# A second feed-forward product by Strassen's identity over column pairs, row pairs and halves, with the residual kept in DRAM

## The chip, the core and the metric

The kernel runs on one NeuronCore of a Trainium2 chip. The metric is the device time of one execution in microseconds; the kernel before takes 2701.98 us (median of three runs, 2699.76 to 2704.55). Besides the runs that were timed there is one profiled execution, with every instruction's start and end.

## What is computed

A trunk of two layers works on x, 1024 frames by 1024 features, in float32. Layer 0 has a convolution module, layer 1 a chunkwise retention; each is followed by a feed-forward of 1024 to 4096 to 1024 features, and an RMS norm ends the trunk. Every sub-layer is normalized and modulated (shift, scale, gate) by a vector made of c. The part that matters here is the last feed-forward:

```python
h = modulate(rmsnorm(x, norm_mlp_g[i]), sh2, sc2)
x = x + g2[:, None, :] * (jnp.square(jax.nn.relu(h @ mlp_w1[i])) @ mlp_w2[i])
...
return rmsnorm(x, final_norm_g)
```

## The kernel before

**Layout.** Everything is held transposed: 128 features on the partitions, frames in the free dimension. x is eight rows of tiles (n = 0 to 7, of 128 features each) by two halves (t = 0 and 1, of 512 frames each), 128x512 apiece, in SBUF under the tags `x0` and `x1`.

**Products.** A float32 operand is split in two float32r tiles, hi (a cast by ScalarE) and lo (a subtraction by VectorE). A product of a 128x128 weight tile and a 128x512 tile is three matmuls into one PSUM bank: hi by hi, hi by lo, lo by hi (`mm3`, lines 258 to 260). `block` (lines 239 to 246) loads 128x1024 weights by SyncE into one of two `raw` buffers and splits them into two `whl` tiles.

**The feed-forward** (`mlp`, lines 416 to 454). The 4096 hidden features are eight blocks of 512. For each block the *first product* makes four hidden tiles for each half (eight times three matmuls each), squares their Relu (ScalarE and VectorE) and splits them (`split_pack`). The *second product* takes the block's four weight tiles of w2, one for each pair of columns (a column is 128 output features, n), and sums for each column and half four times three matmuls in PSUM. VectorE then adds the result, times the gate g2, to x in place (line 454). A block thus has 192 matmuls in each of its two products. PSUM has six buffers `mm` for products and two, `ax`, for norms.

**Order of the blocks in layer 1.** Block 0 runs for half 0 alone, then blocks 1 to 7 for both halves, then block 0 for half 1 alone: there, while the first product runs, the final norm of half 0 is done (`final`), and the second product is cut in 256 columns of frames (`mlp_split`, line 467), each of which is followed by its final norm. The norm of half 1 ahead of block 1 is made by `norm`.

**What sets the order.** The program names the operations in turn; a scheduler of the framework then places each engine's instructions by its own model of their times, and each engine runs its list in order. A tile gets one of the buffers of its tag, and waits for all that used that buffer before. The seven blocks' pools hold 8 `whl`, 16 `hB` (the h of half 1), and 5 each of `hid0` and `hid1`; `tmp` has 4 buffers.

Of the kernel before, what the change touches and what calls it, by code (L numbers as in the profile page):

```python
# [6 lines left out]
F32 = mybir.dt.float32  # L7
# [6 lines left out]
P = 128  # L14
# [192 lines left out]
class Trunk:  # L207
# [209 lines left out]
    def mlp(self, layer, sched, h, g2, mid=None, split=None):  # L417
        nc, io = self.nc, self.io
        for fb, halves in sched:
            hid = {t: [] for t in halves}  # L420
            for f in range(4):
                w = self.block(io["w1"][layer, fb * 4 + f])
                if self.bg:
                    self.bg.pop(0)()
                for t in halves:
                    ps = self.psum()
                    for kt in range(KT):
                        self.mm3(ps, w, kt * P, h[t][kt], kt == 0, kt == KT - 1)
# [3 lines left out]
                    nc.scalar.activation(rl, ps, AF.Relu)  # L432
                    sq = self.t2("tmp")
                    nc.vector.scalar_tensor_tensor(sq, ps, 0.0, rl, ALU.max, ALU.mult)
                    tag = self.hidtag[t]
                    hid[t].append(self.split_from(sq, *tag) if len(tag) == 2 else self.split_pack(sq, *tag))
            if mid is not None:
                mid()
            if split is not None:
                self.mlp_split(layer, fb, halves[0], hid[halves[0]], g2, split)  # L440
                continue
            for np_ in range(4):
                w = self.block(io["w2"][layer, fb, np_])
                if self.bg:
                    self.bg.pop(0)()
                for n2 in range(2):
                    n = np_ * 2 + n2
                    for t in halves:
                        ps = self.psum()
                        for kt in range(4):  # L450
                            o = kt * 256 + n2 * P
                            self.mm3(ps, w, o, hid[t][kt], kt == 0, kt == 3)
                        x = self.x[n][t]
                        nc.vector.scalar_tensor_tensor(x, ps, g2[:, n : n + 1], x, ALU.mult, ALU.add)  # L454

    def mlp_split(self, layer, fb, t, hid, g2, done):

        nc = self.nc
        ws = [self.block(self.io["w2"][layer, fb, np_]) for np_ in range(4)]
        for cs in (slice(0, MID), slice(MID, HALF)):  # L460
            for n in range(KT):
                ps = self.psum()[:, :MID]
                for kt in range(4):
                    o = kt * 256 + n % 2 * P
                    self.mm3(ps, ws[n // 2], o, [a[:, cs] for a in hid[kt]], kt == 0, kt == 3)
                x = self.x[n][t][:, cs]
                nc.vector.scalar_tensor_tensor(x, ps, g2[:, n : n + 1], x, ALU.mult, ALU.add)
            done(t, cs)


    def layer_conv(self):
# [324 lines left out]
        def mlp(fb, p):  # L796
            h = hcols("m0")
            hid = []
            for f in range(4):
                name, ps = ("w1", fb, f), ("psm", fb, f)  # L800
                for kt in range(KT):
                    mm(ps, name, kt * P, h[kt], kt == 0, kt == KT - 1, p)
                rl, hd = ("rl", fb, f), ("hid", fb, f)
                op("A", 0.478, p, lambda ps=ps, rl=rl: nc.scalar.activation(E[rl], E[ps], AF.Relu), r=[ps], w=[rl], a={rl: ("tmp", {})})
                op("V", 0.602, p, lambda ps=ps, rl=rl: nc.vector.scalar_tensor_tensor(E[ps], E[ps], 0.0, E[rl], ALU.max, ALU.mult),
                   r=[rl], w=[ps])
                op("A", 0.478, p, lambda ps=ps, hd=hd: nc.scalar.copy(E[hd][:, :HALF], E[ps]), r=[ps], w=[hd],
                   a={hd: ("hid0", dict(dt=F32R, cols=2 * HALF))})
# [351 lines left out]
    def run(self):  # L1160
        nc, io, tc, main, ctx = self.nc, self.io, self.tc, self.main, self.ctx
        self.x = [[None, None] for _ in range(KT)]
        self.tags = {"raw": (main, RINGS["raw"]), "tmp": (main, RINGS["tmp"]), "rs": (main, 1), "hA": (main, 16),
                     "x0": (main, 8), "x1": (main, 8), "sm": (main, 6)}
        modp = tc.tile_pool(name="modp", bufs=1)
        mp = modp.__enter__()
        self.tags.update(cond=(mp, 1), araw=(mp, RINGS["araw"]))
        self.constants()
        with tc.tile_pool(name="g0", bufs=1) as gp:
            self.tags.update(hB=(gp, 16), hid0=(gp, RINGS["hid0"]), whl=(gp, RINGS["whl"]))  # L1170
            with ExitStack() as self.cstack, tc.tile_pool(name="psc", bufs=1, space=PSUM) as self.ps:
                self.psb = {"mm": 4, "ax": 1, "acc": 3}
                self.hidtag = {0: ["hid0"]}
                hm, g2 = self.layer_conv()
            psp = tc.tile_pool(name="ps", bufs=1, space=PSUM, reuse_waits="tile")
            self.ps = ctx.enter_context(psp)
            self.psb = {"mm": 6, "ax": 2}
            with tc.tile_pool(name="hid", bufs=1) as hp:
                self.tags["hid1"] = (hp, 4)
                self.hidtag = {0: ["hid0"], 1: ["hid1"]}  # L1180
                h, (sh1, G1, g1, sh2, G2, g2) = self.layer_mlp0(hm, g2)
        modp.__exit__(None, None, None)
        with tc.tile_pool(name="ret", bufs=1, reuse_waits="tile") as rp, tc.tile_pool(name="dp", bufs=1, space=bass.MemoryType.DRAM) as dp:
# [7 lines left out]
            self.mlp(1, [(0, [0])], hm, g2, mid=out)  # L1191
        with tc.tile_pool(name="g1", bufs=1, reuse_waits="tile") as gp:
            self.tags.update(whl=(gp, 8), hB=(gp, 16), hid0=(gp, 5), hid1=(gp, 5))
            self.hidtag = {0: ["hid0"], 1: ["hid1"]}
            hm[1] = self.norm(1, G2, sh2, "hB")
            self.mlp(1, [(fb, [0, 1]) for fb in range(1, 8)], hm, g2)

            def first():
                self.tagname = {"tmp": "hid0", "xg": "hA"}
                self.final(0)  # L1200
                self.tagname = {}

# [35 lines left out]
def lay_out(i):  # L1238
# [11 lines left out]
    def kblocks(w):  # L1250

        k, nn = w.shape
        return w.reshape(k // 512, 4, P, 4, 256).transpose(0, 3, 2, 1, 4).reshape(k // 512, 4, P, 1024)

    vec = np.zeros((P, NVEC), np.float32)

    def put(name, a):
# [29 lines left out]
        "w2": c(np.stack([kblocks(w) for w in i["mlp_w2"]])),  # L1287
    }
    d.update(constants_np())
    return d  # L1290
# [23 lines left out]
```

## Time and profile before

| | us |
|---|---|
| runs timed | 2699.76, 2701.98, 2704.55 |
| the profiled execution | 2705.48 |
| its span, first to last instruction | 2703.6 |
| TensorE busy | 2613.8 (97%) |
| VectorE busy | 1635.2 (60%) |
| ScalarE busy | 1068.3 (40%) |
| GpSimd busy | 314.5 (12%) |

The mean granted TensorE clock is 0.985. In the profile PE is TensorE, PEld its weight loads, DVE is VectorE, ACT ScalarE, POOL GpSimd, SP SyncE. A row of the groups reads: line, engine, operation, output and inputs, shapes, count, then busy time and the mean duration in ns, then the idle time of the engine just before and what ended it. A row of the windows gives the stretch and, for each engine, busy time and count. A row of the timeline begins with the start, in us from the first instruction, and the duration. Matmuls are pipelined, so that a matmul's own duration is longer than its share of the time; the distance of starts counts.

### The profile page before, as it was taken

What the parts mean: (1) busy time and instruction counts of PE and PEld (TensorE: products, weight loads), DVE (VectorE), ACT (ScalarE), POOL (GpSimd) and SP (SyncE); (2) the same over time, 40 slices, a digit from 0 to 9 for tenths busy, and PEclk for the clock granted to TensorE, in tenths of its full rate; (3) what the DMA queues carried; (4) which work ended last, traced back from release to release, by engine and by line L of the source; (5) the groups of instructions that cost most, each with busy time, mean ns of one, the idle gap of its engine ahead of it and who ended that gap; (6) DMA issues with size and microseconds to landing.
All of it is one profiled execution on the core that took longest, in us unless ns stands there. A gap on an engine that the chain in (4) does not pass through costs nothing.

```text
span 2703.6 us, 29259 instructions
## 1 busy us (share of the span) xinstructions
PE 2613.8 (97%) x11450; PEld 2119.2 (78%) x11450; DVE 1635.2 (60%) x2237; ACT 1068.3 (40%) x1582; POOL 314.5 (12%) x212
## 2 busy tenths in 40 slices
PE   2989999999999999999999999999999999999997
PEld 1756777888787888788888888888888888888886
DVE  7799999965577445645545655365565333333336
ACT  4656866463222323343433633433543211222124
POOL 3677439100000000000000000000000000000002
PEclk6999999999999999999999999999999999999999
DMA  7522322242376223322222232232222111111112
GB/s 253 203 71 86 109 93 87 93 128 98 119 233 217 96 94 96 115 86 94 71 94 94 71 103 85 71 101 86 78 70 71 48 54 47 47 47 47 48 54 86
DMA packets 77197, 259.66 MB, mean 96 GB/s; under 512 B 8577, under 2 KB 11009, under 8 KB 76930
## 3 DMA queue, kind: packets, MB, share of 16 engines
q1 hardware_dynamic: 74240, 252.98, 28.6%
q10 hardware_dynamic: 2818, 4.81, 0.5%
q8 instruction: 90, 1.47, 0.2%
q14 instruction: 49, 0.40, 0.0%
HBM read 251.46 MB, written 6.29 MB: 95 GB/s over the span
## 4 chain that ended last, share of the span: by engine, by line
PE 84%; DVE 7%; DMA 4%; ACT 2%; issue 2%; POOL 1%; DVEq 0%; ACTq 0%; SPq 0%; POOLq 0%
PE mm L260 25%; PE mm L259 25%; PE mm L258 25%; DMA araw<-ada 3%; PE mm L964 2%; PE mm L963 2%; PE mm L962 2%; DVE acc L733 1%; POOL cacc L741 1%; DVE whl L523 1%; DVE araw L319 1%; PE ax L606 1%; PE acc L721 1%; DVE araw L555 0%; DVE hid L555 0%
## 5 line engine op out<-in xcount | busy, mean ns | idle before, releaser
L245 ACT CAST whl<-raw 128x1024 fp32r<-128x1024 f32 x264 | 277.0, 1050 | 809.7 <-PE mm L259 472.3
L246 DVE TENSOR_TENSOR whl<-raw,whl 128x1024 fp32r<-128x1024 f32 x264 | 322.7, 1223 | 403.5 <-ACT whl L245 302.7
L258 PE MATMUL mm<-hA,whl 128*128 128x512 f32 x1200 | 483.2, 403 | 44.5 <-ACT whl L522 41.7
L260 PE MATMUL mm<-hA,whl 128*128 128x512 f32 x1200 | 475.5, 396 | 8.5 <-DVE whl L523 6.3
L259 PE MATMUL mm<-hA,whl 128*128 128x512 f32 x1200 | 476.1, 397 | 1.9 <-DVE hA L542 1.7
L258 PE MATMUL mm<-hid,whl 128*128 128x512 f32 (+1 forms) x1024 | 394.3, 386 | 4.6 <-ACT hid L281 3.0
L259 PE MATMUL mm<-hid,whl 128*128 128x512 f32 (+1 forms) x1024 | 392.8, 384 | 1.1 <-DVE hid L282 1.0
L260 PE MATMUL mm<-hid,whl 128*128 128x512 f32 (+1 forms) x1024 | 392.8, 384 | 0.0
L258 PEld LDWEIGHTS mm<-hA,whl 128*128 128x128 f32 x1200 | 227.7, 190 | 101.3 <-ACT whl L522 43.5
L258 PE MATMUL mm<-hB,whl 128*128 128x512 f32 x704 | 279.3, 397 | 0.0
L260 PEld LDWEIGHTS mm<-hA,whl 128*128 128x128 f32 x1200 | 227.5, 190 | 63.8 <-DVE whl L523 9.8
L259 PE MATMUL mm<-hB,whl 128*128 128x512 f32 x704 | 274.4, 390 | 0.0
L260 PE MATMUL mm<-hB,whl 128*128 128x512 f32 x704 | 274.2, 390 | 0.0
L259 PEld LDWEIGHTS mm<-hA,whl 128*128 128x128 f32 x1200 | 227.6, 190 | 58.7 <-issue 5.3
L454 DVE SCALAR_TENSOR_TENSOR x<-mm,modb,x 128x512 f32<-128x512 f32 x192 | 143.8, 749 | 211.6 <-PE mm L260 211.0
L741 POOL TENSOR_TENSOR cacc<-cacc,prod 128x512 f32<-128x512 f32 x166 | 253.4, 1529 | 112.9 <-ACT prod L738 57.9
L1143 POOL TENSOR_SCALAR hA<-x,vec 128x256 f32<-128x256 f32 (+1 forms) x12 | 7.5, 622 | 2164.3 <-DVE x L454 2143.8
L258 PEld LDWEIGHTS mm<-hid,whl 128*128 128x128 f32 x1024 | 192.9, 189 | 45.6 <-ACT hid L281 5.9
L259 PEld LDWEIGHTS mm<-hid,whl 128*128 128x128 f32 x1024 | 192.9, 188 | 41.3 <-DVE hid L282 2.9
L260 PEld LDWEIGHTS mm<-hid,whl 128*128 128x128 f32 x1024 | 193.1, 189 | 37.1
L733 DVE SCALAR_TENSOR_TENSOR acc<-x,vec,acc 128x512 f32<-128x512 f32 x239 | 166.8, 746 | 2.8 <-PE acc L721 1.9
L259 PEld LDWEIGHTS mm<-hB,whl 128*128 128x128 f32 x704 | 132.2, 188 | 31.3 <-issue 2.9
(233 smaller groups left out, 3776.3 us busy)
## 6 DMA issues: line engine op xcount, KB each, us to landing
raw<-w SPq DMA_DIRECT2D x192, 512.0 KB, 3.5
araw<-ada SPq DMA_DIRECT2D x80, 512.0 KB, 4.3
raw<-pw SPq DMA_DIRECT2D x38, 512.0 KB, 4.1
raw<-rqk SPq DMA_DIRECT2D x32, 512.0 KB, 3.5
raw<-rv SPq DMA_DIRECT2D x32, 512.0 KB, 3.5
raw<-rgate SPq DMA_DIRECT2D x32, 512.0 KB, 3.5
raw<-rout SPq DMA_DIRECT2D x32, 512.0 KB, 3.5
x<-x SPq DMA_DIRECT2D x32, 256.0 KB, 3.2
```

What stands on the lines that cost most here:

```text
L245: nc.scalar.copy(hi[i], raw[:, i * W : i * W + W])
L246: nc.vector.tensor_tensor(lo[i], raw[:, i * W : i * W + W], hi[i].bitcast(F32), ALU.subtract)
L258: nc.tensor.matmul(out, whi, rhi, start=start, stop=False)
L259: nc.tensor.matmul(out, whi, rlo, start=False, stop=False)
L260: self.last_mm = nc.tensor.matmul(out, wlo, rhi, start=False, stop=stop)
L319: i = nc.vector.scalar_tensor_tensor(raw, raw, 1.0, self.cond, ALU.mult, ALU.mult, accum_out=out)
L454: nc.vector.scalar_tensor_tensor(x, ps, g2[:, n : n + 1], x, ALU.mult, ALU.add)
L733: op("V", 0.68, p, lambda s=s, a=a: nc.vector.scalar_tensor_tensor(E[a], sl(s), wv(s), E[a], ALU.mult, ALU.add), r=[u], w=[a])
L741: op("G", 1.28, p, lambda pr=pr: nc.gpsimd.tensor_tensor(E[ca], E[ca], E[pr], ALU.add), r=[pr], w=[ca])
L962: nc.tensor.matmul(vps[jt], hh[0], wh, start=kt == 0, stop=False)
L963: nc.tensor.matmul(vps[jt], hh[0], wl, start=False, stop=False)
L964: nc.tensor.matmul(vps[jt], hh[1], wh, start=False, stop=kt == KT - 1)
```

## The change

In blocks 1 to 7 of the last feed-forward the second product is no longer a sum of plain products. Take a pair of output columns (n1, n2), a pair of hidden tiles (kj = 0, 1) and the two halves: that is a 2x2 by 2x2 product of tiles, and in place of its eight products seven are made, of sums and differences:

A11·B11, A12·B21, S2·T2, S1·T1, S4·B22, S3·T3, A22·T4.

- `pair_weights` loads a column pair's weights (laid out anew by `kpairs`), makes S1 to S4 on VectorE and splits them all: four `whl` tiles a pair.
- In `mlp_seven` the hidden tiles' Relu is done by ScalarE in PSUM and the Square by ScalarE into buffers of `x0`; VectorE makes T1 to T4, and seven tiles of each pair of hidden tiles are split.
- `seven` runs the products over the two pairs of hidden tiles (six matmuls each, in one PSUM bank). The results are gathered, times g2, in tiles of `tmp`: ScalarE makes two (a and b) from the first product, VectorE adds the others, eight additions a pair.
- x no longer lies in SBUF during these blocks: it is stored to DRAM tiles `xd` at the start by SyncE, and each finished 128x512 tile is added to it by a transfer that GpSimd issues (`accum_op=ALU.add`), four a pair. After block 7 it is loaded back: half 0 by SyncE, half 1 by ScalarE's queue.
- Buffers: `whl` 9, `hB` 8 (the other half of half 1's h takes buffers of `x1`), `hid0` 14, a new `q2`.
- `o2` only gives the place of a weight tile in the new layout, for the blocks that are done as before.

The core of the diff:

```diff
+    def pair_weights(self, ap):
+        nc = self.nc
+        tt = nc.vector.tensor_tensor
+        raw = self.t2("raw", cols=1024)
+        nc.sync.dma_start(raw, ap)
+        a11, a12, a21, a22 = (raw[:, i * 256 : i * 256 + 256] for i in range(4))
+        ph, pl, qh, ql = (self.t2("whl", dt=F32R, cols=1024) for _ in range(4))
+        q = self.t2("q2")
+        tt(q[:, 256:], a11, a21, ALU.subtract)
+        nc.scalar.copy(qh[:, 512:768], a22)
+        tt(ql[:, 512:768], a22, qh[:, 512:768].bitcast(F32), ALU.subtract)
+        tt(a21, a21, a22, ALU.add)
+        tt(a22, a21, a11, ALU.subtract)
+        tt(q[:, :256], a12, a22, ALU.subtract)
+        nc.scalar.copy(ph, raw)
+        tt(pl, raw, ph.bitcast(F32), ALU.subtract)
+        nc.scalar.copy(qh[:, :512], q)
+        tt(ql[:, :512], q, qh[:, :512].bitcast(F32), ALU.subtract)
...
+    def seven(self, np_, w, hid, g2, xd):
...
+        def plus(ps, n, e, new=False):
+            o = self.t2("tmp") if new else e
+            nc.vector.scalar_tensor_tensor(o, ps, g(n), e, ALU.mult, ALU.add)
+            return o
+        def done(n, t, e):
+            nc.gpsimd.dma_start(xd[n][t], e, accum_op=ALU.add)
+        ps = prod("A11", "B11")
+        a, b = self.t2("tmp"), self.t2("tmp")
+        nc.scalar.activation(a, ps, AF.Copy, scale=g(n1))
+        nc.scalar.activation(b, ps, AF.Copy, scale=g(n2))
+        done(n1, 0, plus(prod("A12", "B21"), n1, a, True))
+        ps = prod("S2", "T2")
+        plus(ps, n1, a)
+        plus(ps, n2, b)
+        m5 = prod("S1", "T1")
+        plus(m5, n1, a)
+        plus(prod("S4", "B22"), n1, a)
+        done(n1, 1, a)
+        plus(prod("S3", "T3"), n2, b)
+        done(n2, 1, plus(m5, n2, b, True))
+        plus(prod("A22", "T4"), n2, b)
+        done(n2, 0, b)
...
+                        nc.scalar.activation(ps, ps, AF.Relu)
+                        sq = f[kj, t] = self.t2("x0")
+                        nc.scalar.activation(sq, ps, AF.Square)
...
-            self.tags.update(whl=(gp, 8), hB=(gp, 16), hid0=(gp, 5), hid1=(gp, 5))
-            self.hidtag = {0: ["hid0"], 1: ["hid1"]}
-            hm[1] = self.norm(1, G2, sh2, "hB")
-            self.mlp(1, [(fb, [0, 1]) for fb in range(1, 8)], hm, g2)
+            self.tags.update(whl=(gp, 9), hB=(gp, 8), hid0=(gp, 14), q2=(gp, 1))
...
+            for kt in range(KT):
+                nc.sync.dma_start(xd[kt][1], self.x[kt][1])
+                h.append(self.norm_h(1, kt, r, G2[:, kt : kt + 1], sh2[:, kt : kt + 1], "hB" if kt < 4 else "x1"))
...
+                nc.sync.dma_start(xd[kt][0], self.x[kt][0])
+            self.mlp_seven(1, range(1, 8), hm, g2, xd)
...
+                nc.sync.dma_start(self.x[kt][0], xd[kt][0])
...
+                nc.scalar.dma_start(self.x[kt][1], xd[kt][1])
```

Lines of the changed kernel that the prediction names: 497 is `plus`, 505 and 506 the two copies of the first product, 501 the adding transfer, 469 to 478 the weights' sums and splits, 1234 the final norm's sum of squares (1132 before), 569 the addition in `mlp_split` (467 before), 439 and 287 the square and the split of a hidden tile in `mlp` (434 and 282 before). The order of an engine's instructions is shown with each tile's number, in the form line, operation, output<-inputs, shape.

More of the change, by code (lines that the diff above doesn't have):

```diff
@@ L28, with o2 @@
 VEC = {}
+def o2(kt, n):
+    return (n % 2 * 4 + kt % 2 * 2 + kt // 2) * P
 def _vec_layout():
@@ new lines, in seven, with prod @@
+    def seven(self, np_, w, hid, g2, xd):
+        nc = self.nc
+        n1, n2 = 2 * np_, 2 * np_ + 1
+        g = lambda n: g2[:, n : n + 1]
+        def prod(a, k):
+            ps = self.psum()
+            wt, o = w[a]
+            for p in range(2):
+                self.mm3(ps, wt, o + p * P, hid[p][k], p == 0, p == 1)
+            return ps
+        def plus(ps, n, e, new=False):
[20 more added lines that the diff above has]
+        done(n2, 0, b)
@@ new lines, in mlp_seven @@
+    def mlp_seven(self, layer, fbs, h, g2, xd):
+        nc, io = self.nc, self.io
+        tt = nc.vector.tensor_tensor
+        for fb in fbs:
+            hid = []
+            for p in range(2):
+                f = {}
+                ops = {}
+                pack = lambda k, src: ops.update({k: self.split_pack(src, "hid0")})
+                for kj in range(2):
+                    w = self.block(io["w1"][layer, fb * 4 + 2 * p + kj])
+                    for t in range(2):
+                        ps = self.psum()
+                        for kt in range(KT):
+                            self.mm3(ps, w, kt * P, h[t][kt], kt == 0, kt == KT - 1)
+                        nc.scalar.activation(ps, ps, AF.Relu)
+                        sq = f[kj, t] = self.t2("x0")
+                        nc.scalar.activation(sq, ps, AF.Square)
+                        if (kj, t) == (0, 0):
+                            pack("B11", sq)
+                        elif (kj, t) == (0, 1):
+                            tt(f[0, 0], sq, f[0, 0], ALU.subtract)
+                            pack("T1", f[0, 0])
+                        elif (kj, t) == (1, 0):
+                            pack("B21", sq)
+                        else:
+                            pack("B22", sq)
+                            tt(f[0, 0], sq, f[0, 0], ALU.subtract)
+                            pack("T2", f[0, 0])
+                            tt(f[0, 1], sq, f[0, 1], ALU.subtract)
+                            pack("T3", f[0, 1])
+                            tt(f[1, 0], f[1, 0], f[0, 0], ALU.subtract)
+                            pack("T4", f[1, 0])
+                hid.append(ops)
+            for np_ in range(4):
+                self.seven(np_, self.pair_weights(io["w2"][layer, fb, np_]), hid, g2, xd)
@@ L463, in mlp_split @@
                 for kt in range(4):
-                    o = kt * 256 + n % 2 * P
-                    self.mm3(ps, ws[n // 2], o, [a[:, cs] for a in hid[kt]], kt == 0, kt == 3)
+                    self.mm3(ps, ws[n // 2], o2(kt, n), [a[:, cs] for a in hid[kt]], kt == 0, kt == 3)
                 x = self.x[n][t][:, cs]
@@ L1191, in run @@
             self.mlp(1, [(0, [0])], hm, g2, mid=out)
+        xp = ctx.enter_context(tc.tile_pool(name="xd", bufs=1, space=bass.MemoryType.DRAM))
         with tc.tile_pool(name="g1", bufs=1, reuse_waits="tile") as gp:
-            self.tags.update(whl=(gp, 8), hB=(gp, 16), hid0=(gp, 5), hid1=(gp, 5))
-            self.hidtag = {0: ["hid0"], 1: ["hid1"]}
-            hm[1] = self.norm(1, G2, sh2, "hB")
-            self.mlp(1, [(fb, [0, 1]) for fb in range(1, 8)], hm, g2)
+            self.tags.update(whl=(gp, 9), hB=(gp, 8), hid0=(gp, 14), q2=(gp, 1))
+            self.hidtag = {1: ["hid0"]}
+            xd = [[xp.tile([P, HALF], F32, name=self.nm("xd"), tag=f"xd{n}_{t}") for t in range(2)] for n in range(KT)]
+            r = self.norm_rstd(1)
+            h = []
+            for kt in range(KT):
+                nc.sync.dma_start(xd[kt][1], self.x[kt][1])
+                h.append(self.norm_h(1, kt, r, G2[:, kt : kt + 1], sh2[:, kt : kt + 1], "hB" if kt < 4 else "x1"))
+            hm[1] = h
+            for kt in range(KT):
+                nc.sync.dma_start(xd[kt][0], self.x[kt][0])
+            self.mlp_seven(1, range(1, 8), hm, g2, xd)
+            xl = [self.t2("hid0", cols=2 * HALF) for _ in range(4)]
+            for kt in range(KT):
+                self.x[kt][0] = self.t2("x0")
+                nc.sync.dma_start(self.x[kt][0], xd[kt][0])
+            for kt in range(KT):
+                self.x[kt][1] = xl[kt // 2][:, kt % 2 * HALF : kt % 2 * HALF + HALF]
+                nc.scalar.dma_start(self.x[kt][1], xd[kt][1])
             def first():
@@ L1286, in lay_out @@
         "w1": c(np.stack([ktiles(w, 0) for w in i["mlp_w1"]])),
-        "w2": c(np.stack([kblocks(w) for w in i["mlp_w2"]])),
+        "w2": c(np.stack([kpairs(w) for w in i["mlp_w2"]])),
     }
```

10 lines of the change are left out of this document (7 added, 3 removed).

## Prediction

> **What bounds the kernel now.** I read the page first: the shares of the engines and the chain that ended last.
>
> ```profile
> PE 2613.8 (97%) x11450; PEld 2119.2 (78%) x11450; DVE 1635.2 (60%) x2237; ACT 1068.3 (40%) x1582; POOL 314.5 (12%) x212
> ...
> PE 84%; DVE 7%; DMA 4%; ACT 2%; issue 2%; POOL 1%; DVEq 0%; ACTq 0%; SPq 0%; POOLq 0%
> ```
>
> TensorE is the bound almost everywhere. Then the stage itself, by windows: one second product and the first product after it, in the middle of the seven blocks, then the last block's first product (half 1 alone) and the end.
>
> ```profile
> core 0: us, PE busy (x) PEld busy (x) DVE busy (x) ACT busy (x) POOL busy (x), PEclk, DMA share, GB/s
> 2071.50:2115.00 43.50, 43.50 (x193) 36.02 (x193) 17.36 (x21) 5.31 (x6) 0.00 (x0) 1.00 0.16 49
> 2115.00:2159.20 44.20, 44.20 (x193) 36.05 (x193) 15.07 (x19) 12.43 (x18) 0.00 (x0) 1.00 0.15 48
> 2641.30:2663.00 21.70, 21.70 (x97) 18.00 (x96) 11.86 (x15) 9.86 (x14) 0.00 (x0) 1.00 0.23 73
> 2663.00:2703.60 40.60, 26.87 (x203) 24.89 (x202) 30.05 (x50) 16.17 (x36) 13.74 (x14) 0.91 0.30 105
> ```
>
> In the blocks PE has no gap and the full granted clock; VectorE is at 34 to 40%, GpSimd idle. Only the last 40.6 us are not PE's: there VectorE is busy for 30.05.
>
> **The gain.** A second product is 192 matmuls (the 193 counts one that straddles the edge) in 43.5 us, 0.2267 us each. The change runs 7 of 8 products: 4 column pairs x 42 = 168 per block, 24 fewer, 168 fewer over seven blocks: 168 x 0.2267 = **38.1 us**. A product of six matmuls takes 1.36 us, a column pair 9.52, a block's second product 38.1. First products stay.
>
> **What VectorE gets.** Prices from the rows of the stage (busy) and from a dense stretch elsewhere (start to start):
>
> ```profile
> L454 DVE SCALAR_TENSOR_TENSOR x<-mm,modb,x 128x512 f32<-128x512 f32 x96 | 72.0, 750 | 150.0 <-PE mm L260 149.8
> L246 DVE TENSOR_TENSOR whl<-raw,whl 128x1024 fp32r<-128x1024 f32 x50 | 61.2, 1225 | 95.6 <-ACT whl L245 92.8
> L282 DVE TENSOR_TENSOR hid<-tmp,hid 128x512 fp32r<-128x512 f32 x50 | 34.6, 691 | 30.2 <-ACT hid L281 30.2
> L281 ACT CAST hid<-tmp 128x512 fp32r<-128x512 f32 x50 | 31.0, 621 | 53.7 <-DVE tmp L434 53.7
> L432 ACT ACTIVATE tmp<-mm 128x512 f32<-128x512 f32 x51 | 30.4, 596 | 72.1 <-PE mm L260 72.1
> ```
>
> ```profile
> 1560.89 0.68 DVE L270 TENSOR_TENSOR q<-tmp,q 128x512 fp32r<-128x512 f32 x1
> 1561.49 0.68 DVE L917 TENSOR_TENSOR tmp<-mm,cs 128x512 f32<-128x512 f32 x1
> ...
> 1564.49 0.74 DVE L1082 SCALAR_TENSOR_TENSOR x<-mm,modb,x 128x512 f32<-128x512 f32 x1
> 1565.15 0.68 DVE L270 TENSOR_TENSOR k<-tmp,k 128x512 fp32r<-128x512 f32 x1
> ...
> 1569.27 1.22 DVE L246 TENSOR_TENSOR whl<-raw,whl 128x1024 fp32r<-128x1024 f32 x1
> 1570.40 1.28 DVE L270 TENSOR_TENSOR st<-tmp,st 128x512 fp32r<-128x512 f32 x2
> ```
>
> ```profile
> L374 DVE TENSOR_TENSOR rs<-hid,hid 128x256 f32<-128x256 f32 x2 | 0.8, 424 | 0.2
> ```
>
> Back to back, instructions overlap: an addition of a product 0.66 us, a 512-column operation 0.60, a 1024-column one 1.13; a 256-column one 0.34 (0.42 less the same overlap, an estimate). A column pair now needs 8 additions (5.28) where it had 4, and for its weights 1.13 + 0.60 + 5 x 0.34 = 3.43 where it had 1.13: **8.7 us of VectorE for 9.52 of PE**. That fits, with little to spare. The first product, 44.2 us of PE, carries 14 splits and 8 differences of 0.60, two pairs' weights and little else, some 22 us. ScalarE has per pair two copies of a product (0.6 each) and 2 us of casts: hidden.
>
> At the turn from first to second product T2 of the last hidden tile is late: Relu and square (0.6 each), difference 0.66, cast 0.62, low part 0.69, with one copy ahead of the cast in ScalarE's order, about 4.2 us; PE comes to it after three products, 4.1 us. I put 0.3 us a block: **2 us**.
>
> **The wait that is added.** A finished tile leaves through a transfer issued by GpSimd that adds to DRAM; its `tmp` buffer, one of four, is free when that has landed. Of VectorE's order around a pair's end, before (two columns of two halves each):
>
> ```order
> L454 SCALAR_TENSOR_TENSOR x1_912_4310<-mm_3287_16278,modb_1523_7887,x1_912_4310 128x512
> L246 TENSOR_TENSOR whl_3315_16489<-raw_3313_16486,whl_3314_16488 128x1024
> L454 SCALAR_TENSOR_TENSOR x0_515_2224<-mm_3291_16298,modb_1523_7887,x0_515_2224 128x512
> L454 SCALAR_TENSOR_TENSOR x1_913_4319<-mm_3292_16312,modb_1523_7887,x1_913_4319 128x512
> L454 SCALAR_TENSOR_TENSOR x0_518_2233<-mm_3293_16326,modb_1523_7887,x0_518_2233 128x512
> ```
>
> And now, from the second pair's end into the third (tmp_3578, written first, is the tile whose buffer tmp_3590 takes):
>
> ```order
> L497 SCALAR_TENSOR_TENSOR tmp_3578_17750<-mm_3575_17725,modb_1523_7887,tmp_3571_17703 128x512
> L473 TENSOR_TENSOR raw_3597_17846<-raw_3597_17846 128x256
> L497 SCALAR_TENSOR_TENSOR tmp_3571_17703<-mm_3579_17753,modb_1523_7887,tmp_3571_17703 128x512
> L474 TENSOR_TENSOR q2_3602_17852<-raw_3597_17846 128x256
> L476 TENSOR_TENSOR whl_3599_17849<-raw_3597_17846,whl_3598_17848 128x1024
> L497 SCALAR_TENSOR_TENSOR tmp_3590_17797<-mm_3589_17790,modb_1523_7887,tmp_3587_17786 128x512
> L478 TENSOR_TENSOR whl_3601_17851<-q2_3602_17852,whl_3600_17850 128x512
> ```
>
> Between the tile and the one that needs its buffer lie 0.34 + 0.66 + 0.34 + 1.13 = 2.5 us of work. Call L the time from the end of the addition to the buffer's release. No row of before shows a GpSimd transfer or one that adds; the nearest, of the same 256 KB:
>
> ```profile
> raw<-w SPq DMA_DIRECT2D x192, 512.0 KB, 3.5
> ...
> std<-tmp SPq DMA_DIRECT2D x8, 256.0 KB, 2.0
> tmp<-std SPq DMA_DIRECT2D x8, 256.0 KB, 2.6
> ```
>
> ```profile
> 2249.26 0.33 SPq L239 DMA_DIRECT2D raw<-w  x1
> ```
>
> ```profile
> L1151 POOL TENSOR_TENSOR hA<-hA,rs 128x512 f32<-128x512 f32 x3 | 4.7, 1593 | 27.7 <-DVE rs L374 27.7
> ```
>
> Lower end: a plain store, 2.0, issued in 0.33, and 0.15 for the semaphore: 2.5 us. Upper end: a load and then a store, 4.6, and GpSimd as long over the issue as over its 1.59 us operation: 6.3. I take 4.2, near the middle: the read and the write of different rows overlap.
>
> How much L may be: let t = 0 be PE's end of the first product. After Relu and Square VectorE starts at 1.5 on three differences, four low parts (two of which wait for casts), a 256-column operation and the first addition; they end at 6.9. Six more additions of 0.66 end at 10.9: there the first pair's last new tile is complete. Pair 2 can begin at 10.9 + L (for L over 3), needs 7 x 0.66 + 3 x 0.34 = 5.7 to its own last new tile; pair 3, with two weight blocks of 1.13 among its additions, 7.5. So pair 4's first addition begins at 10.9 + 5.7 + 7.5 + 3L = 24.1 + 3L and frees its PSUM buffer at 24.8 + 3L. PE has six PSUM buffers; it wants that one for the next block at 28 x 1.36 + 0.2 = 38.3. **L up to 4.5 us costs nothing; every us beyond costs 3 us a block, 21 us in all.** At 4.2 I leave 0.4 us a block for transfers that land late: **3 us**.
>
> "DMA: Bandwidth & Descriptors" of the Trainium skill, section "Anatomy of one DMA — SWDGE (gpsimd) path", gives 2.0 us + bytes/436e3, by which 256 KB take 2.6 us (an estimate; it speaks of plain transfers) and the ring would cost 0; no run so far shows it.
>
> **The two seams.** At the start, 16 stores of x stand among SyncE's weight loads; the second weight tile waits only for columns 0 and 1, done 15 us earlier, the third for the block's end, 22 us ahead of its use. Half 1's h partly lies in buffers of x: half a first-product group may run at another pace (rival 3): **1 us**. At the end the residual of half 0 comes back by loads, and its final norm, which ran beside the last first product, moves behind it. VectorE before, from the last hidden tile:
>
> ```order
> L434 SCALAR_TENSOR_TENSOR tmp_3688_19203<-mm_3686_19176,tmp_3687_19201 128x512
> L370 SCALAR_TENSOR_TENSOR hid0_3717_19263<-ax_3690_19208,hid0_3716_19261 128x512
> L282 TENSOR_TENSOR hid1_3689_19205<-tmp_3688_19203,hid1_3689_19205 128x512
> L372 TENSOR_SCALAR hid0_3718_19265<-hid0_3717_19263 128x512
> L374 TENSOR_TENSOR rs_3719_19267<-hid0_3718_19265,hid0_3715_19259 128x512
> ```
>
> And now: the sums of squares (L1234) only begin there.
>
> ```order
> L439 SCALAR_TENSOR_TENSOR tmp_3982_20007<-mm_3980_19980,tmp_3981_20005 128x512
> L287 TENSOR_TENSOR hid0_3983_20009<-tmp_3982_20007,hid0_3983_20009 128x512
> L1234 TENSOR_TENSOR hid0_3987_20017<-hid0_3985_20013,hid0_3986_20015 128x512
> L569 SCALAR_TENSOR_TENSOR hid0_3944_19832<-mm_4026_20113,modb_1523_7887,hid0_3944_19832 128x256
> L1234 TENSOR_TENSOR hid0_3989_20021<-hid0_3987_20017,hid0_3988_20019 128x512
> ```
>
> ```profile
> 2668.17 0.69 DVE L374 TENSOR_TENSOR rs<-hid,hid 128x512 f32<-128x512 f32 x1
> 2668.78 0.48 DVE L467 SCALAR_TENSOR_TENSOR x<-mm,modb,x 128x256 f32<-128x256 f32 x1
> 2669.18 6.29 DVE L1151 TENSOR_TENSOR hA<-hA,rs 128x512 f32<-128x512 f32 x5
> 2675.39 0.86 DVE L467 SCALAR_TENSOR_TENSOR x<-mm,modb,x 128x256 f32<-128x256 f32 x2
> ```
>
> ```profile
> 2696.65 0.42 DVE L374 TENSOR_TENSOR rs<-hid,hid 128x256 f32<-128x256 f32 x1
> 2697.11 2.96 DVE L1155 TENSOR_TENSOR hA<-hA,rs 128x512 f32<-128x512 f32 x3
> ```
>
> Before, half 0's `rs` is ready 5.9 us after PE's 2663.0 and the block of five multiplications (6.3 us) delays the additions of the first 256 columns; the last `rs` ends 34.1 after. Now eight squares (ScalarE, from 2.2, 0.55 apart) and seven sums (0.60) go between the eight additions that PE paces, 12 x 0.12 us a column of 256, to 12.2; three steps each on ScalarE and VectorE give `rs` at about 15.3; the five multiplications end at 22, the late additions of the second 256 columns, among the sums of the first, at 26.9; then one norm chain after the other, 3 us to an `rs`, 5 with two multiplications beside GpSimd and four sums, 3 more: the last `rs` at about 37.5. **3.5 us**, between 1 and 7.
>
> **Sum.** -38.1 + 2 + 3 + 1 + 3.5 = -28.6, about **29 us**. The profiled execution took 2705.48 us (span 2703.6, 1.9 around it), 3.5 over the median of 2701.98; the saving is a count of matmuls and holds for either: 2701.98 - 29 = **2673 us**. The unknowns of this case give 2666 to 2681.
>
> **Rivals.**
> 1. *The ring binds a little*, L from 4.5 to 6.0: at 5.3, 24.8 + 15.9 - 38.3 = 2.4 us a block, 17 in place of the 3: 2687. For it: VectorE has no slack to catch up inside a block. Chance 0.14.
> 2. *The ring binds wholly: slower.* At L = 6.0 it costs 4.5 us a block, 32 in all, and with the 6.5 of the other terms the gain is gone; at 7.5 it is 9.0 a block, 63 in all: 2733. For it: the upper end of my rows, 6.3, is there already, and the loads share the engines. Against: nothing in the blocks moves over 49 GB/s now. Chance 0.16.
> 3. *PE's pace.* First and second products have as many matmuls, 44.2 against 43.5 us: some tiles stream slower, by up to 0.7/96 = 0.007 us. If all new tiles did, 1176 x 0.007 = 8 us: 2681. Chance 0.06.
> 4. *GpSimd's work slows VectorE.* The five multiplications above took 6.29 us for 5 x 0.60 while GpSimd ran three: about 1.1 us each that met one. If issuing a transfer does that to each SBUF-to-SBUF operation that it meets (40% of VectorE's time), 4 x 0.4 x 1.1 = 1.8 us a pair, 10.5 against 9.52, up to 27 us, of which the PSUM buffers take some: 2690 to 2700. Chance 0.06.
>
> The trace has only GpSimd reading SBUF beside VectorE. The Trainium skill's "SBUF — State Buffer", section "Who interferes with whom", says that a two-input VectorE operation collides with GpSimd instructions that read SBUF, and not with those that only write, as descriptor generation (inferred there): by it rival 4 costs 0. The 6.29 us row agrees with its first half; no run here shows the second.
>
> **Numbers.** My case 0.58. The range reaches up into rivals 1 and 4: 2666 to 2700. A measurement of this kernel tells 0.2% (5.4 us) from no change: faster 0.79 (my case, rival 3, most of 1 and 4), same 0.07 (their rest and the edge of 2), slower 0.14.
>
> **What would show it.** In the seven blocks: 168 fewer matmuls, second product 38 to 39 us, VectorE near 90% in it, PE's idle time by DVE and ACT under 1.5 us a block. L: issue to landing of the transfers to `xd`, under 4.5 with the issue; VectorE or ScalarE waiting on DMA ahead of L497, L505 or L506 speaks for rivals 1 and 2. At the end: 42 to 47 us from the last first product to the end of the span. I am wrong if PE waits at each block's end for a PSUM buffer, or if L497 and the 256-column operations run longer than 0.75 and 0.42 us.

## The result and the profile after

The changed kernel takes 2726.51 us (median of 4 runs, 2720.23 to 2729.57); the kernel before took 2702.78 beside it (2699.76 to 2704.55). The ratio is 1.0086, with a 95% interval of 1.0066 to 1.0106: slower by 0.9%, where 1% faster was forecast.

The page of the changed kernel: the engines' busy time, the DMA queues (packets, MB, share of the time of 16 DMA engines), and two rows of the groups.

```profile
PE 2595.9 (95%) x11282; PEld 2090.6 (77%) x11282; DVE 1794.3 (66%) x2559; ACT 1180.3 (43%) x1792; POOL 414.7 (15%) x324
...
q1 hardware_dynamic: 77696, 259.27, 30.4%
q0 software_dynamic: 16128, 29.37, 7.7%
...
L501 POOL DMA_DIRECT2D xd<-tmp x112 | 97.7, 920 | 2056.8 <-DVE tmp L497 2056.0
...
L497 DVE SCALAR_TENSOR_TENSOR tmp<-mm,modb,tmp 128x512 f32<-128x512 f32 x224 | 157.2, 743 | 64.1 <-DMA xd<-tmp 58.8
```

The 168 matmuls are gone (11450 to 11282) and VectorE's additions cost what was forecast (743 ns each). What is new stands at the end of the last row: VectorE idles 58.8 us for adding transfers; ScalarE's copies, which need buffers of the same ring, wait 28.0 us for them too, ahead of L506. The same four windows as before, shifted to where the stages now lie (second product, first product, last first product, end):

```profile
core 0: us, PE busy (x) PEld busy (x) DVE busy (x) ACT busy (x) POOL busy (x), PEclk, DMA share, GB/s
2157.80:2201.40 43.60, 40.19 (x169) 31.16 (x167) 32.16 (x48) 16.37 (x24) 10.43 (x12) 0.98 0.72 139
2201.40:2246.70 45.30, 45.30 (x193) 36.82 (x193) 23.20 (x39) 17.68 (x30) 3.48 (x4) 0.98 0.26 53
2640.90:2665.90 25.00, 24.97 (x96) 20.27 (x97) 13.05 (x16) 7.92 (x11) 5.86 (x6) 0.88 0.84 222
2665.90:2724.00 58.10, 29.86 (x203) 27.07 (x201) 36.86 (x60) 22.79 (x48) 14.44 (x14) 0.81 0.23 81
```

A second product of 168 matmuls still takes 43.6 us, because PE is busy for only 40.2 of them (some of that at half pace) where 38.3 was to be had. The DMA engines are busy for 72% of it, after 16%. The end takes 58.1 us in place of 40.6 (40.1 counted, as below, from PE's first start in it). VectorE's timeline around the turn from one column pair to the next in block 3, and GpSimd's beside it:

```profile
2257.91 0.74 DVE L497 SCALAR_TENSOR_TENSOR tmp<-mm,modb,tmp 128x512 f32<-128x512 f32 x1
...
2263.21 0.75 DVE L497 SCALAR_TENSOR_TENSOR tmp<-mm,modb,tmp 128x512 f32<-128x512 f32 x1 [1.63 <-DMA xd<-tmp]
...
2273.42 0.75 DVE L497 SCALAR_TENSOR_TENSOR tmp<-mm,modb,tmp 128x512 f32<-128x512 f32 x1 [1.83 <-DMA xd<-tmp]
...
2287.84 4.83 DVE L497 SCALAR_TENSOR_TENSOR tmp<-mm,modb,tmp 128x512 f32<-128x512 f32 x7 [4.22 <-DMA xd<-tmp]
```

```profile
2253.06 0.86 POOL L501 DMA_DIRECT2D xd<-tmp  x1 [44.64 <-DVE tmp L497]
2257.30 2.64 POOL L501 DMA_DIRECT2D xd<-tmp  x3 [3.37 <-DVE tmp L497]
2264.26 0.86 POOL L501 DMA_DIRECT2D xd<-tmp  x1 [4.32 <-DVE tmp L497]
```

The first addition of pairs 2, 3 and 4 each waits for a transfer of the pair before, 1.6, 1.8 and 4.2 us, as the prediction's rule has it. The second fence tells why: the first tile's transfer goes out alone, the last two or three of a pair together. Taken from each transfer's landing less the end of the addition that finished its tile, L over all 28 pairs is 4.3 us in the mean for the first tile of a pair, 5.0, 6.5 and 7.4 for the second to the fourth. The first addition of pairs 2, 3 and 4 starts within 0.13 us of the landing of the third tile of the pair before.

Where the 20.4 us between the two profiled spans (2703.6 and 2724.0) lie, in PE's starts: the seven blocks 616.0 us against 615.5 (577.4 without the 168 matmuls); the last first product 25.0 against 22.2; from its end to the end of the span 58.1 against 40.1; and 0.9 less ahead of the blocks. So some 38 us were lost inside the blocks and 21 behind them.

### The profile page after: what moved, and what is told of

Read it like the earlier page. It is cut to its first block, busy times and chain, and to the rows that moved or that the text cites. A ratio compares the mean times of both kernels' runs of the same rounds, so it can differ in the third digit from the quotient of the medians.

```text
span 2724.0 us, 29902 instructions
## 1 busy us (share of the span) xinstructions
PE 2595.9 (95%) x11282; PEld 2090.6 (77%) x11282; DVE 1794.3 (66%) x2559; ACT 1180.3 (43%) x1792; POOL 414.7 (15%) x324
## 3 DMA queue, kind: packets, MB, share of 16 engines
q0 software_dynamic: 16128, 29.37, 7.7%
## 4 chain that ended last, share of the span: by engine, by line
PE 62%; issue 20%; DVE 6%; DMA 5%; POOL 4%; ACT 2%; DVEq 0%; POOLq 0%; ACTq 0%; SPq 0%
PE mm L264 18%; PE mm L265 18%; PE mm L263 18%; POOL xd L501 3%; PE mm L1066 2%; PE mm L1064 2%; PE mm L1065 2%; DMA araw<-ada 2%; DMA xd<-tmp 1%; DVE acc L835 1%; PE acc L823 1%; DVE araw L324 1%; PE ax L708 1%; POOL cacc L843 1%; DVE whl L625 1%
## 5 line engine op out<-in xcount | busy, mean ns | idle before, releaser
L263 PE MATMUL mm<-hA,whl 128*128 128x512 f32 x1200 | 484.5, 404 | 48.6 <-ACT whl L624 40.7
L251 DVE TENSOR_TENSOR whl<-raw,whl 128x1024 fp32r<-128x1024 f32 x236 | 288.0, 1221 | 305.7 <-ACT whl L250 210.7
L250 ACT CAST whl<-raw 128x1024 fp32r<-128x1024 f32 x236 | 247.6, 1050 | 538.4 <-PE mm L264 155.6
L501 POOL DMA_DIRECT2D xd<-tmp x112 | 97.7, 920 | 2056.8 <-DVE tmp L497 2056.0
L263 PE MATMUL mm<-hid,whl 128*128 128x512 f32 (+1 forms) x968 | 374.5, 389 | 23.9 <-ACT tmp L506 9.7
L264 PE MATMUL mm<-hid,whl 128*128 128x512 f32 (+1 forms) x968 | 372.9, 387 | 1.8 <-DVE hid L287 1.8
L265 PE MATMUL mm<-hid,whl 128*128 128x512 f32 (+1 forms) x968 | 371.4, 385 | 0.3 <-DVE whl L476 0.3
L264 PEld LDWEIGHTS mm<-hA,whl 128*128 128x128 f32 x1200 | 228.4, 190 | 58.1 <-issue 5.1
L263 PEld LDWEIGHTS mm<-hid,whl 128*128 128x128 f32 x968 | 182.5, 189 | 71.8 <-ACT tmp L506 12.7
L263 PE MATMUL mm<-hB,whl 128*128 128x512 f32 x576 | 230.7, 400 | 3.3 <-DVE tmp L497 3.3
L264 PE MATMUL mm<-hB,whl 128*128 128x512 f32 x576 | 226.0, 392 | 0.0
L265 PE MATMUL mm<-hB,whl 128*128 128x512 f32 x576 | 225.9, 392 | 0.0
L264 PEld LDWEIGHTS mm<-hid,whl 128*128 128x128 f32 x968 | 183.3, 189 | 41.3 <-DVE hid L287 5.9
L265 PEld LDWEIGHTS mm<-hid,whl 128*128 128x128 f32 x968 | 183.6, 190 | 36.1 <-DVE whl L476 0.8
L497 DVE SCALAR_TENSOR_TENSOR tmp<-mm,modb,tmp 128x512 f32<-128x512 f32 x224 | 157.2, 743 | 64.1 <-DMA xd<-tmp 58.8
L625 DVE TENSOR_TENSOR whl<-raw,whl 128x1024 fp32r<-128x1024 f32 x92 | 123.5, 1349 | 36.2 <-PE mm L264 10.9
```

The lines of the kernel that those rows point to most:

```text
L250: nc.scalar.copy(hi[i], raw[:, i * W : i * W + W])
L251: nc.vector.tensor_tensor(lo[i], raw[:, i * W : i * W + W], hi[i].bitcast(F32), ALU.subtract)
L263: nc.tensor.matmul(out, whi, rhi, start=start, stop=False)
L264: nc.tensor.matmul(out, whi, rlo, start=False, stop=False)
L265: self.last_mm = nc.tensor.matmul(out, wlo, rhi, start=False, stop=stop)
L497: nc.vector.scalar_tensor_tensor(o, ps, g(n), e, ALU.mult, ALU.add)
```

## The experiments

Nine kernels, each made from the changed one. The table gives the four numbers to which the expectations speak; the stretches come from PE's starts in the profiled execution, so that the start of the blocks, which varies by up to 7 us between the profiled executions (2019.9 to 2026.8), is left out. "Period" is the time from one block's second product to the next one's, the mean of the first five. Each ratio is to runs of the kernel before taken beside that kernel (medians of 2701.2 to 2703.4).

| kernel | median us | ratio to before (95%) | period | seven blocks | last first product | end |
|---|---|---|---|---|---|---|
| before | 2702.8 | 1 | 87.7 | 615.5 | 22.2 | 40.1 |
| changed | 2726.5 | 1.0086 (1.0066, 1.0106) | 87.7 | 616.0 | 25.0 | 58.1 |
| e1 ring of 8 | 2690.5 | 0.9949 (0.9934, 0.9964) | 82.6 | 584.6 | 22.0 | 56.9 |
| e2 no transfer | 2674.0 | 0.9895 (0.9878, 0.9911) | 82.6 | 579.8 | 22.0 | 49.2 |
| e3 plain store | 2691.1 | 0.9953 (0.9938, 0.9968) | 82.6 | 581.6 | 22.1 | 59.9 |
| e4 six blocks | 2715.9 | 1.0045 (1.0028, 1.0063) | 87.7 | 615.8 | 22.0 | 51.1 |
| e5 ring of 6 | 2691.5 (one run) | | 82.6 | 584.5 | 22.0 | 57.7 |
| e6 norm's own buffers | 2719.2 | 1.0071 (1.0051, 1.0091) | 87.9 | 618.0 | 27.4 | 49.8 |
| e7 ring of 8, norm's own | 2683.6 | 0.9939 (0.9923, 0.9956) | 82.6 | 584.9 | 23.6 | 48.6 |
| e8 the same, six blocks | 2675.7 | 0.9906 (0.9891, 0.9920) | 82.6 | 585.7 | 22.4 | 41.8 |
| e9 the same, last block in SBUF | 2671.2 | 0.9887 (0.9870, 0.9903) | 82.6 | 579.7 | 22.4 | 42.8 |

### e1: a ring of eight

```diff
-            o = self.t2("tmp") if new else e
+            o = self.t2("res") if new else e
...
-            self.tags.update(whl=(gp, 9), hB=(gp, 8), hid0=(gp, 14), q2=(gp, 1))
+            self.tags.update(whl=(gp, 9), hB=(gp, 8), hid0=(gp, 14), q2=(gp, 1), res=(gp, 4))
```

> Four more buffers for finished tiles: the two new tiles of a column pair come from a ring of four of their own, a and b keep the old ring of four, so that a buffer is wanted again two pairs after its transfer was issued. Theory A (the ring of four binds, because a buffer is released some 5.5 us after its addition): VectorE's wait at the gathering line for the adding transfers (58.8 us between 2030 and 2660) falls under 10 us and the seven blocks shrink from 616 to 580 to 592 us; total 2690 to 2703. Theory B (the transfers' load on the DMA engines makes the weight loads late, whatever the ring): the waits move to the weights' casts and the blocks stay within 5 us of 616; total 2722 to 2730. Theory C (VectorE has too much work in the second product): no wait for a transfer is left, VectorE is busy without a gap in the second products and the blocks stay above 605.

Theory A. A second product, and the first product after it:

```profile
2148.90:2187.20 38.30, 38.30 (x169) 31.38 (x168) 35.19 (x53) 15.20 (x24) 11.30 (x13) 1.00 0.80 151
2187.20:2231.50 44.30, 44.30 (x193) 36.04 (x192) 20.67 (x35) 18.31 (x31) 2.59 (x3) 1.00 0.26 61
```

None of VectorE's waits for adding transfers is left. PE has no gap in the second product, at the full clock; VectorE is busy for 35.2 of 38.3 us, near the 90% of the prediction, and that holds. Theory B falls on two rows of the DMA issues (KB each, median us to landing; 2100 to 2560), of the changed kernel and of this one:

```profile
raw<-w SPq DMA_DIRECT2D x44, 512.0 KB, 5.6
```

```profile
raw<-w SPq DMA_DIRECT2D x43, 512.0 KB, 5.7
```

The weights land as late as in the changed kernel (3.5 before the change), and PE does not notice. The transfers themselves are no faster either (L is 6.2 us in the mean, after 5.8): more buffers hide the latency, they don't shorten it.

### e2 and e3: no transfer, and one that doesn't add

```diff
-            nc.gpsimd.dma_start(xd[n][t], e, accum_op=ALU.add)
+            pass                               # e2
+            nc.gpsimd.dma_start(xd[n][t], e)   # e3
```

> No transfer adds to DRAM: what the seven blocks contribute to x is left out, all the arithmetic of the products stays. Theory A and theory B: both lose their cause, the seven blocks take 578 to 586 us (615.5 less 38.1, plus 1 to 8 for the turn from the first to the second product), total 2684 to 2694 if the end stays as late as it is. Theory C (VectorE has too much work): the blocks stay above 605 us.

> The same transfers, issued by the same engine, store without adding: the blocks' contributions overwrite x in DRAM, the sum is left out. Theory A with the adding as the cause of the late release: issue to landing falls from 5.3 to 2.5 to 3.5 us, the release to about 3.5 to 4 us, under the 4.5 of the prediction's rule; blocks 580 to 592 us, weight loads land in 3.5 to 4 us in place of 5.6. If it is the issue by GpSimd that is slow and not the adding: landing stays above 4.5 us and the blocks above 605.

Both as theory A has it, and C falls: without a transfer the seven blocks take 579.8 us, 2.4 over a bare 577.4. PE's starts say where these 2.4 lie: 0.24 in each second product, with two longer steps at its third and fourth product, where the turn's last sums are due (1.7 in all; the prediction had 2), and 0.15 in each first product but the first. The total was lower than expected because the end also gained, 49.2 in place of 58.1. In e3 the ring is of four and the blocks are as fast, which the prediction's rule wants: L is 3.5 us, and the weights land in 3.7. Queue and transfer of e3's page:

```profile
q0 software_dynamic: 8960, 29.37, 2.8%
...
L501 POOL DMA_DIRECT2D xd<-tmp x112 | 60.8, 543 | 2061.3 <-DVE tmp L497 2059.8
...
xd<-tmp POOLq DMA_DIRECT2D x112, 256.0 KB, 2.7
```

and the last row's counterpart on the page of the changed kernel:

```profile
xd<-tmp POOLq DMA_DIRECT2D x112, 256.0 KB, 5.3
```

For the same bytes the adding transfer needs 1.8 times the packets, occupies the 16 DMA engines for 1.87 us (7.7% of 2724 over 112) in place of 0.67 (2.8% of 2688), keeps GpSimd busy for 0.87 us (97.7 over 112) in place of 0.54, and lands in 5.3 us in place of 2.7. The 2.6 us that the Trainium skill's "DMA: Bandwidth & Descriptors" (section "Anatomy of one DMA — SWDGE (gpsimd) path") gives (an estimate by its formula) fits the plain transfer of e3, 2.7; the adding one is twice that.

### e5: a ring of six

```diff
+            ... q2=(gp, 1), res=(gp, 2))
```

> As the ring of eight, but the two new tiles of a pair share two buffers of their own instead of four: six in all. By the prediction's rule, carried over (a new tile's buffer is wanted again one column pair later, 9.5 us less one addition of 0.7): L up to 8.8 us costs nothing. Theory A (the ring alone binds, at L of 4.5 to 6.9 as the changed kernel's trace shows): blocks of 82.6 to 83.2 us as with eight buffers, total 2686 to 2696. If the ring of eight helped because two pairs' time lies between, not one: blocks of 84 to 87 us, total above 2700.

(`plus` takes `res` here as in e1.) The period is that of e1 (82.63 us, after 82.66): the time of one pair is enough of a delay, and two buffers more would have done. It is one run.

### e4 and e6: the end

```diff
-            self.mlp_seven(1, range(1, 8), hm, g2, xd)
+            self.mlp_seven(1, range(1, 7), hm, g2, xd)
...                                            # x is loaded back here, as before
+            self.hidtag = {0: ["hid0"], 1: ["hid0"]}
+            self.mlp(1, [(7, [0, 1])], hm, g2)
```

> Blocks 1 to 6 as in the changed kernel; x is loaded back after block 6, and block 7 is a plain feed-forward into SBUF, so that the last adding transfers and the reload lie a whole block (88 us) ahead of the end. Theory D (the end is late because the reload of x stands between the last block and the final norm and holds up ScalarE and the weights): the last first product goes back from 25.0 to about 22 us and the stretch after it from 58.1 to 40 to 46; total 2704 to 2714. Theory E (the end is late because the hidden tiles and the final norm's tiles share one ring, which puts the norm's squares behind the last hidden tile whatever the reload does): the stretch after it stays above 50 us; total 2716 to 2726. GpSimd's closing drain (8.8 us) should shrink, as its last transfer is long done.

```diff
             def first():
-                self.tagname = {"tmp": "hid0", "xg": "hA"}
+                self.tagname = {"tmp": "fin", "xg": "hA"}   # fin: 4 buffers of its own
```

> The changed kernel with one edit: the temporaries of half 0's final norm get four buffers of their own in place of the hidden tiles' ring; the ring of finished tiles stays at four. Theory E (the shared ring puts the norm's squares behind the last hidden tile): they come before it again, the stretch after the last first product falls from 58.1 to 42 to 50 us. Theory D (the late reload itself holds the end up): the squares, earlier in ScalarE's order, now wait there for x and hold up the casts behind them; block 7 or the last first product grows by what the end gains, total within 6 us of 2726. The seven blocks stay at 87.5 us each for both, so the total is 2708 to 2718 by E alone.

Neither theory alone. With x back a block earlier (e4) the end falls, as D wants, but only to 51.1, as E wants. The last first product is 22.0 again; that decides nothing, since it is 22.0 in e1 too, where the reload is late. ScalarE's order around the last hidden tile, in the changed kernel and then in e4, shows E's part:

```profile
2656.17 0.60 ACT L437 ACTIVATE tmp<-mm 128x512 f32<-128x512 f32 x1 [6.77 <-DMA xd<-tmp]
...
2672.98 0.62 ACT L286 CAST hid<-tmp 128x512 fp32r<-128x512 f32 x1 [2.00 <-DVE tmp L439]
2673.50 2.19 ACT L1227 ACTIVATE hid<-x 128x512 f32<-128x512 f32 x4
```

```profile
2663.80 0.62 ACT L286 CAST hid<-tmp 128x512 fp32r<-128x512 f32 x1 [0.97 <-DVE tmp L439]
2664.32 2.19 ACT L1227 ACTIVATE hid<-x 128x512 f32<-128x512 f32 x4
```

The squares of half 0's norm (L1227) begin only behind the cast of the last hidden tile, 7.6 us after the first product's end in the changed kernel, although the last load of half 0 was issued at 2657, and 2.4 after it in e4, where nothing is loaded late. With buffers of their own (e6) they come before it and the end falls to 49.8; but x is late, so they and the squares of the hidden tiles wait there: the last first product takes 27.4 us and the blocks 2.0 more. Of the 8.3 gained 4.4 are given back. E's 2708 to 2718 is missed by a little (2719.2).

GpSimd's closing drain (its wait at the program's end) hardly shrank in e4, 7.5 us after 8.8, though its last transfer had landed 138 us earlier; that expectation was wrong. What it goes with is the number of GpSimd's transfers: 7.5 us for 96 (e4, e8), 8.1 for 104 (e9), 8.8 for the 112 of each other kernel that adds; with e3's 112 plain ones it is 11.0. Why, no run shows. In e2, with no GpSimd transfer at all, it takes 1.8 us, as before the change. The span ends 3.6 us after SyncE's drain in the changed kernel and 0.7 before: 2.9 us, a price of having used such transfers at all (1.6 in e4).

### e7 to e9: both together

e7 is e1 with half 0's norm in the buffers `res`; e8 is e7 with e4's edit. e9 keeps seven blocks:

```diff
         def done(n, t, e):
+            if last:
+                x = self.x[n][t]
+                nc.gpsimd.tensor_tensor(x, x, e, ALU.add)
+                return
...
+            last = fb == fbs[-1]
+            for kt in range(KT if last else 0):
+                self.x[kt] = [self.t2("x0"), self.t2("hA")]
+                nc.sync.dma_start(self.x[kt][0], xd[kt][0])
+                nc.gpsimd.dma_start(self.x[kt][1], xd[kt][1])
```

> Ring of eight, and half 0's final norm takes its temporaries from the four buffers of the finished new tiles. By E alone: blocks 82.6 us, stretch after the last first product 42 to 48 us in place of 56.9: total 2676 to 2682. By D: the last first product or its start grows, as x comes back only after the last adding transfers (2624 with the ring of eight, first product from 2605.6 to 2627.6); total 2683 to 2692.

> Ring of eight, blocks 1 to 6 by seven products, x back after block 6, block 7 plain, half 0's final norm with temporaries of its own: takes away the ring, the late reload and the late norm together. Six blocks of 82.6 and one of 87.7 us, the last first product 22 us, the end as before the change (40.5 us) plus 0 to 3 for GpSimd's drain: span 2668 to 2672, total 2669 to 2676, 27 to 34 us under before. If D and E are both incomplete (the loads from DRAM disturb something else), the stretch after the last first product stays above 46 us and the total above 2680.

> Ring of eight and the norm's own temporaries; all seven blocks by seven products; block 7 alone adds no tile in DRAM: x is loaded back while its second product starts (half 0 into the squares' buffers, half 1 into those of half 0's h, both free by then), and GpSimd adds each finished tile to it in SBUF, 16 additions of some 1.6 us. Theory A, D and E together: blocks as without any adding transfer, 579.8 us for the seven, the last first product 22, the end 41 to 43: span 2663 to 2669, total 2665 to 2671, some 6 us under the version with a plain block 7. Rival (GpSimd's additions slow VectorE's two-input operations in block 7, as its multiplications do in the final norm: 6.3 us for five of 0.6): block 7's second product takes 45 to 55 us and the total is 2674 to 2685.

e7, at 2683.6 us in D's range, shows D's part once the ring is out of the way: 48.6 us at the end. In e1 and e7 another 5 us go at the turn into the last first product (584.6 and 584.9 against 579.8). SyncE's issues in e1 there, then ScalarE's order, then PE:

```profile
2580.09 12.37 SPq L1311 DMA_DIRECT2D x<-xd  x3
2592.56 0.37 SPq L244 DMA_DIRECT2D raw<-w  x1
```

```profile
2598.26 1.04 ACT L250 CAST whl<-raw 128x1024 fp32r<-128x1024 f32 x1 [7.28 <-DMA raw<-w]
...
2600.40 0.68 ACT L506 ACTIVATE tmp<-mm,modb 128x512 f32<-128x512 f32 x1
```

```profile
2601.13 0.62 PE L263 MATMUL mm<-hid,whl 128*128 128x512 f32 x1 [2.71 <-ACT tmp L506]
```

The loads of x stand in SyncE's queue and wait there for the last adding transfers; a weight load is stuck behind them, ScalarE waits 7.3 us for it with the copy of a product behind, and PE waits for that copy; behind the wait come eight matmuls at half pace (0.43 us apart in place of 0.23), some 1.7 of the 5 us. In e8, where no reload is near, the end is 41.8; the total is in the expected range, while the span of the profiled execution, 2676.7, is above the expected 2668 to 2672: its blocks began the latest of all, at 2026.8. In e9 nothing is added in DRAM in block 7; its second product, the last first product and the end:

```profile
2562.00:2600.90 38.90, 38.90 (x172) 31.88 (x171) 37.68 (x51) 17.09 (x26) 22.09 (x16) 1.00 0.29 95
2600.90:2623.30 22.40, 22.40 (x98) 18.20 (x97) 19.28 (x23) 14.91 (x22) 6.81 (x5) 1.00 0.33 94
2623.30:2666.10 42.80, 28.21 (x202) 26.09 (x200) 29.83 (x50) 14.66 (x35) 14.39 (x14) 0.84 0.28 99
```

All three stretches are those expected. GpSimd's 16 additions did not slow VectorE enough to reach PE, so that the rival of this expectation falls. At 2671.2 us, 31.7 under before and 4.5 under e8 (some 6 were expected), e9 is the fastest of these kernels; the span, 2666.1, lies in the expected range and the median 0.2 us above it.

## Why the prediction was wrong

**What held.** 168 matmuls fewer. VectorE's prices: 743 ns an addition (746 in e2, where GpSimd issues nothing). The operations from SBUF to SBUF, of which rival 4 speaks, are no slower for GpSimd's transfers either: 419 to 422 ns at 256 columns against 420 to 426 in e2, 687 against 689 at 512 (L287), so that rival 4 falls. The rule of the Trainium skill's "SBUF — State Buffer" (section "Who interferes with whom"), by which a two-input VectorE operation does not collide with descriptor generation (inferred there), agrees. The turn: 1.7 us for the seven, 2 forecast. Rival 3 falls but for a small rest: in e2 the second product's matmuls start 0.227 us apart outside the turn, as before the change, and 0.15 us in each of six first products, 0.9, is what is left of its 8. And the rule held on both sides: with L = 3.5 (e3) four buffers cost nothing (82.6 us a block); in the changed kernel the third tile of a pair, whose buffer is the one wanted, has an L of 5.8, 5.2 and 6.7 us after the first, second and third pair, 17.7 together where 13.5 were free: 4.2 us a block by the rule, 5.1 measured (87.7 less 82.65).

**The step that failed first: "I take 4.2, near the middle".** A transfer that goes out alone has that price: the first tile's L is 4.3 us in the mean, 4.0 at least (whether reads and writes of different rows overlap in it, the prediction's reason, no run shows). But four leave in each 9.5 us, two or three of them back to back, and each occupies all the DMA engines for 1.87 us: 7.5 of 9.5. L grows along the burst, from 4.3 to 7.4, as of transfers that queue, and the tile on which the ring turns is the third of them. The prediction had bounds for one transfer from rows of one transfer, and weighed no load; its argument against rival 2 ("nothing in the blocks moves over 49 GB/s now") read the bytes, while an adding transfer takes the engines 2.8 times as long for a byte as a plain one. So "3 us" for the ring was 36: 5.1 in each of seven blocks, which is rival 1's mechanism at an L just under its upper end (5.9 in the mean of the three), and near rival 2's threshold; the outcome, slower, is rival 2's, at a chance of 0.16. The rule also left out ScalarE's copies, which wait for the second tile of the pair before (28.0 us) and end some of PE's waits.

Some gaps also cost PE more than themselves, which may be most of the 0.9 that the rule lacks. PE's timeline in the changed kernel, at the end of block 2's second product:

```profile
2196.98 0.39 PE L265 MATMUL mm<-hid,whl 128*128 128x512 f32 x1
2199.22 0.50 PE L263 MATMUL mm<-hid,whl 128*128 128x512 f32 x1 [1.86 <-ACT tmp L506]
...
2200.47 0.63 PE L264 MATMUL mm<-hid,whl 128*128 128x512 f32 x1
2200.90 0.63 PE L265 MATMUL mm<-hid,whl 128*128 128x512 f32 x1
...
2203.33 0.43 PE L264 MATMUL mm<-hA,whl 128*128 128x512 f32 x1
2203.60 0.39 PE L265 MATMUL mm<-hA,whl 128*128 128x512 f32 x1
```

A wait of 2.2 us from start to start, and from 2200.0 to 2203.3 matmuls start 0.43 us apart or more, not 0.227. Windows of the changed kernel give the granted clock (the number behind the engines) there, behind a longer wait, and in the last first product:

```profile
2200.00:2203.40 3.40, 3.40 (x9) 2.22 (x8) 2.71 (x4) 0.40 (x2) 0.86 (x1) 0.50 0.76 212
2375.30:2381.40 6.10, 3.72 (x16) 2.75 (x15) 4.12 (x7) 1.44 (x2) 0.88 (x1) 1.00 0.57 129
2640.30:2647.10 6.80, 6.17 (x15) 4.88 (x16) 6.71 (x10) 1.99 (x2) 1.17 (x2) 0.50 0.89 258
```

Of the five ends of a second product in the period's mean, three come with such a stretch at half the clock: their first products take 1.2, 1.0 and 1.7 us more than e2's 44.1, the other two 0.1 each, 0.8 us a block. The Trainium skill's "TensorE: Matmul & The Clock Gate" (section "Part 1: The HAM clock gate (the "warmup" mystery)") gives 426.7 ns for a 512-column matmul on a cold array, which the trace confirms, and an idle window of about 3.4 us ahead of it; here one wait of 2.2 us, with three of 0.65 to 1.18 in the ten before, was enough, while behind one of 2.8 (the second window) PE kept its pace, as behind one of 3.5 in e4 (2548.5). The length of a wait alone doesn't decide it; what does, these runs leave open.

**The second: "3.5 us, between 1 and 7" for the end.** It was 18.0. Three things, which the runs separate:
- The norm's place: 9.1 us (e2, with neither late loads nor the drain, has 49.2 against 40.1). The working was right within a microsecond up to the first `rs` of half 1 (29.9 forecast, 30.7 us after the first product's end in e2); it failed behind that, where it gave 8 us to the last `rs`, which came 12 later: PE's sums over partitions, 3.0 us from VectorE's last sum to ScalarE's next step, were not in it.
- The late reload: some 6 us more (58.1 less 49.2 and less the drain; 6.8 by e7 less e8), since weights and casts wait behind it in the queues of SyncE and ScalarE. The prediction named the loads and no wait for them; the last turn alone takes 5 us in e1.
- GpSimd's drain: 2.9 us, in no term.

The last first product, 2.8 us longer, holds no wait at all. It runs at half the clock from 2640.3 to 2647.1 (the third window above), behind the wait of 3.7 us at the turn, which the addition of a tile of block 7's last pair ended: that addition had waited 6.4 us for a transfer, after 3.2 to 4.7 in the other blocks. With more buffers (e1, e5) or without adding (e2, e3) the last first product takes 22.0 or 22.1.

Summed from the profiles: -38.1 + 2.4 that e2 keeps + 36.2 in the blocks and the last turn + 2.8 + 18.0 - 0.9 = 20.4 us, the difference of the spans. What stays open is why the adding transfer needs the DMA engines so much longer; the packets (16128 against 8960) suggest that the destination is read as well, but no run showed that.

## What to carry to other kernels

Price a buffer ring by the latency of the transfer under the load that the change itself makes, of that tile in a burst on which the ring turns and not of one alone: bytes per second don't show it, the time that the DMA engines are busy does. Where a ring binds, two more buffers may be worth as much as a transfer twice as fast (e5 and e3 take the same time). When data is moved out to DRAM, its way back is part of the change: a load that waits stops everything behind it in the queue of the engine that issues it, so let it wait on an engine with nothing else to do, or make it early enough not to wait.

## What the runs showed of the hardware

- A GpSimd transfer that adds to DRAM (128x512 float32): 0.87 us of GpSimd to issue, 5.3 to land, 1.87 us of all 16 DMA engines; without adding 0.54, 2.7 and 0.67.
- After a wait of 2.2 us PE ran at half pace (0.43 us a matmul, granted clock 0.5) for some 3 us, and after one of 3.7 us for some 6; after others, of 2.8 and 3.5 us, it did not.
- Once GpSimd has issued transfers, its drain at the program's end takes 7.5 (96 transfers) to 8.8 us (112), 11.0 with 112 plain ones, instead of 1.8, even where the last landed 138 us before.
